# Ten of 22 pairs of the last product with seven block products, their weight sums made earlier and kept in DRAM

## The chip, the cores and the metric

The kernel runs on one core of one Trainium2 chip. The metric is the device time of one execution in microseconds (us). Several runs were timed; their median counts. One more execution was recorded by the hardware profiler, and all views below come from it.

## The reference, cut to what matters

One decoder block on 256 tokens of width 2048, in float32: a norm, two token mixers side by side, an output projection with a residual, then a SwiGLU feed-forward and a final norm. The change concerns the feed-forward alone:

```
h2 = rms_norm(x, norm2_w)                                   # 256 x 2048
x  = x + (silu(h2 @ w_gate) * (h2 @ w_up)) @ w_down         # 5632 wide inside
return rms_norm(x, norm_f_w)
```

`w_gate` and `w_up` are 2048 x 5632, `w_down` is 5632 x 2048. The last product, with `w_down`, is the one that is changed.

## The kernel before, in words

**Three matmuls for one.** Each float32 operand is held as a sum of two parts that TensorE multiplies at its full rate: `hi`, a rounded copy, and `lo`, the rest. A product is hi*hi + hi*lo + lo*hi, so three matmuls stand for each block product. Weights come raw from DRAM and are split in place of use: ScalarE writes `hi` (L161, and L1356 in the last product), VectorE then `lo` = raw - hi (L162, L1357). The tiles `hi` and `lo` are rings of `NH` = 3 buffers of 1024 columns each; a buffer is written again when TensorE has gone through the matmuls that read it. The raw weights lie in a ring of 3 buffers of 2048 columns (1 MB), which SP loads.

**Who sets the order.** The program emits instructions in the order of the code, and a planner then orders each engine's queue by priority and by when it expects the operands. Splits carry a raised priority (`high_priority`), so they run ahead of other work; `pin` keeps an instruction at its place in program order. Side work is written as generators: `add` puts one in a lane, and `pump`, called after each half chunk of weights, advances it by one `yield`.

**Gate/up stage** (L1253 on). For each of 22 groups `g` of 256 inner features, `group_t` computes the gate and the up product, transposed: 256 features by 256 tokens. Four half chunks for each of the two, 24 matmuls of 256 columns per half chunk (L238). The result goes to VectorE (`sgt`), then to one of two places: for a *plain* group, to a hi/lo pair of tiles in `fa`; for a group in `SEVEN` (six of the 22, g = 12 to 17), as float32 into a tile `pairs`.

**Last product** (L1360 on). Two passes p, one for each half of 1024 output columns; a pass runs over the 22 groups ("pairs" of two 128-row blocks of `w_down`).

- A plain pair: four output blocks (two token halves, two column halves c of 512) and two k blocks, three matmuls each, 24 matmuls of 512 columns. They come as two plain halves of 12 (`plain_half`), each with one split of 1024 columns.
- A pair in `SEVEN`: the 2x2 block product by the scheme of Strassen and Winograd, with seven block products instead of eight, 21 matmuls. It needs sums of the left blocks (`sums4`, `sums`, collected by `lefts` into the tiles `left[i]`) and of the weight blocks. `seven_of` makes the weight sums there and then: `d13` on VectorE (L1450), `d24` in two steps on GpSimd (L1451, L1452). It goes in four pieces of 6, 3, 6 and 6 matmuls, and `units` puts a plain half behind each, so that one seven pair is spread over two plain pairs. The products p1, p5, p6, p7 have PSUM banks of their own, which add up over all pairs of a pass.
- The bank set of the products of pass 0 serves pass 1 as accumulators, so `early` empties it at the end of pass 0 into `x1`. `weighted` (L1509) runs in pass 1 on the columns finished in pass 0.
- At the end of pass 1 the splits of the last two plain pairs are made first (`tail`), then their matmuls run sorted by token half, so that the final norm of the first half can start (`add`, `square`, `factor`, `scaled`, L1555 on). One of these splits has a buffer of its own instead of a place in the ring.

Of the kernel before, what the change touches and what calls it, by code (L numbers as in the profile page):

```python
# [7 lines left out]
F32 = mybir.dt.float32  # L8
# [6 lines left out]
P = 128  # L15
# [6 lines left out]
SEVEN = (12, 13, 14, 15, 16, 17)  # L22
# [75 lines left out]
class Kern:  # L98
# [26 lines left out]

    def load(self, src, w, nk=4, parts=None):
        nc = self.nc
        raw = self.wp.tile([P, 2048], F32, tag="raw", bufs=3, name=self.nm("raw"))
        rv = raw[:, :nk * w].rearrange("p (k n) -> p k n", n=w)
        if parts:  # L130

            for i, (k0, k1) in enumerate(parts):
                self.on_load(k0, k1)
                (nc.scalar if i < 2 else nc.sync).dma_start(rv[:, k0:k1, :], src[:, k0:k1, :])
        else:
            nc.sync.dma_start(rv, src)
        return rv

    def split_one(self, rv, w, h, ahead):
# [6 lines left out]
        with self.tc.high_priority(offset=self.HP):  # L146
            for k in range(2):
                self.pin(nc.scalar.activation(hv[:, k, :], rv[:, 2 * h + k, :], AF.Copy))  # L148
                ahead(2 * h + k)
                self.pin(nc.vector.tensor_tensor(lv[:, k, :], rv[:, 2 * h + k, :], hv[:, k, :].bitcast(F32), op=OP.subtract))  # L150
        return hv, lv

    def split(self, rv, w, h, o=0):
        nc = self.nc
        m = rv.shape[1] // 2
# [4 lines left out]
        with self.tc.high_priority(offset=self.HP):  # L160
            nc.scalar.activation(hv, rv[:, m * h:m * h + m, :], AF.Copy)  # L161
            nc.vector.tensor_tensor(lv, rv[:, m * h:m * h + m, :], hv.bitcast(F32), op=OP.subtract)  # L162
        return hv, lv

    def group(self, srcs, acts, w=512, t_outer=False):
# [10 lines left out]
        for c, src in enumerate(srcs):  # L176
            rv = self.load(src, w)
            for h in range(2):
                hv, lv = self.split(rv, w, h)
# [16 lines left out]
    def pair(self, srcs, acts, ws, first):  # L196
# [4 lines left out]
        for c in range(n):  # L201
            for g in range(2):
# [4 lines left out]
                for h in range(2):  # L207
                    if lead:
                        hv, lv = self.split_one(rv, w, h, first.prep0)
                    else:  # L210
                        if g == 0:
                            first.prep(c, h)
                        hv, lv = self.split(rv, w, h)
# [7 lines left out]
    def group_t(self, srcs, acts, out=None):  # L221
# [6 lines left out]
        for c, src in enumerate(srcs):  # L228
            rv = self.load(src, 256, nk=8)
            for h in range(2):  # L230

                hv, lv = self.split(rv, 256, h, 16 * self.nudge)
# [503 lines left out]
    def nsa_kv(self):  # L736
# [36 lines left out]
        for kind in range(2):  # L773
            bank = self.paux.tile([P, 512], F32, tag="acc", bufs=1, name=self.nm("hid"))
            for u in range(2):
                rv = self.load(self.t["w1"][kind * 2 + u], 512)
                for h in range(2):
                    hv, lv = self.split(rv, 512, h)
# [195 lines left out]
    def build(self):  # L974
# [264 lines left out]

        def sums4():  # L1240

            for _ in range(2):
                yield
# [8 lines left out]
        zt = None  # L1252
        for g in range(2 * NFG):  # L1253
            if g == 2 * NFG - 3:
# [7 lines left out]
            if g in SEVEN:  # L1262
                if zt is None:
                    zt = self.xy.tile([P, ZW], F32, tag="z", name="pairs")
                    fp = [zt[:, 512 * o:512 * o + 512] for o in range(6)]
                    z4 = zt[:, 0:2048].rearrange("p (q k t n) -> p q k t n", q=4, k=2, t=2)
                    s4 = [v7(x[:, k]) for x in (pb.tile([P, 2, 512], F32, name=n, tag=n, bufs=1) for n in ("d13", "d24")) for k in range(2)]
                V.tensor_tensor(fp[SEVEN.index(g)].rearrange("p (k n) -> p k n", k=2), e, sgt[:], op=OP.mult)
# [3 lines left out]
            if q % 2 == 0:  # L1272
# [4 lines left out]
                else:  # L1277
                    j = i // 2 - 2
                    if i % 2 == 0:
# [404 lines left out]
```

## Time and profile before

| | |
|---|---|
| median of 3 runs | 1452.66 us (1452.3 to 1454.12) |
| the profiled execution's own time | 1453.31 us |
| its span, first to last instruction | 1451.5 us |
| mean granted TensorE clock | 0.998 |
| gate/up stage | from about 743.5 us to 1211 us of the span |
| last product, pass 0 and pass 1 | from 1211 us; last matmul about 1443 us |

How to read it: PE is TensorE's matmul queue, PEld its weight loads, DVE VectorE, ACT ScalarE, POOL GpSimd, SP the engine that issues most DMAs. A row of instructions gives line, engine, operation and tiles (out<-in), count, then busy time and mean length. A row of waits says which instruction stood idle and which one released it. A row of windows gives the busy time of each engine in a stretch of the span, the granted clock, the busy share of the 16 DMA engines and what they moved. Matmuls overlap in the pipeline, so the length of one (0.39 us for 512 columns) is longer than the distance from one to the next.

### The profile page before, as it was taken

The page shows a single profiled execution, that of the slowest core. Times are in us where ns is not written, and L with a number is a line of the kernel's source. Part 1 is how long each engine was busy: PE and PEld are TensorE (multiplying, and loading weights), DVE is VectorE, ACT ScalarE, POOL GpSimd, SP SyncE. Part 2 cuts the span into 40 slices and gives each one's busy share as a digit, 9 for nine tenths or more (in the row PEclk, how much of TensorE's full clock was granted, in tenths as well). Part 3 has the DMA queues.
Part 4 walks back from the last instruction along what each step waited for, and adds up shares of the span by engine and source line. Part 5 has one row for each costly group of instructions (what it writes and reads, how often), then busy time and mean ns, then how long its engine had stood idle before and what let it go on. Part 6 is the DMA issues. An engine that isn't in the chain of part 4 may idle for free.

```text
span 1451.5 us, 26237 instructions
## 1 busy us (share of the span) xinstructions
PE 1440.7 (99%) x10991; PEld 1377.7 (95%) x10991; DVE 979.7 (67%) x1430; ACT 713.9 (49%) x887; POOL 114.9 (8%) x86
## 2 busy tenths in 40 slices
PE   9999999999999999999999999999999999999997
PEld 9999999999999999998899999999999998888886
DVE  7678997767687755566565555555554558777877
ACT  6655444355455546444454444444444446555555
POOL 1000101000000000120000000000000002221120
PEclk9999999999999999999999999999999999999999
DMA  8665546345554455555555555555555554656653
GB/s 285 231 214 174 177 163 224 121 146 204 203 194 155 146 204 175 183 198 200 175 193 188 200 195 186 200 195 187 200 196 186 200 201 165 216 198 213 209 193 145
DMA packets 48024, 277.12 MB, mean 191 GB/s; under 512 B 5777, under 2 KB 6305, under 8 KB 22049
## 3 DMA queue, kind: packets, MB, share of 16 engines
q1 hardware_dynamic: 45792, 269.56, 53.4%
q10 hardware_dynamic: 1008, 3.25, 0.6%
q0 software_dynamic: 1104, 2.64, 0.6%
q8 instruction: 86, 1.41, 0.4%
q14 instruction: 34, 0.27, 0.1%
HBM read 272.52 MB, written 2.89 MB: 190 GB/s over the span
## 4 chain that ended last, share of the span: by engine, by line
PE 84%; DVE 3%; DMA 0%; issue 0%; ACT 0%; DVEq 0%; ACTq 0%
PE mm L238 56%; PE mm L1369 5%; PE mm L1370 5%; PE mm L1368 5%; PE mm L266 3%; PE mm L265 3%; PE mm L264 3%; DVE lo L162 1%; PE oacc L931 1%; PE U L601 1%; PE mmx L1369 1%; PE mmx L1370 1%; PE mmx L1368 1%; DVE main L403 0%; DVE xs L497 0%; PE pt L917 0%
## 5 line engine op out<-in xcount | busy, mean ns | idle before, releaser
L162 DVE TENSOR_TENSOR lo<-raw,hi 128x1024 fp32r<-128x1024 f32 (+2 forms) x422 | 508.4, 1206 | 297.6 <-ACT hi L161 296.6
L161 ACT ACTIVATE hi<-raw 128x1024 fp32r<-128x1024 f32 (+2 forms) x422 | 440.3, 1046 | 501.6 <-PE mm L238 386.2
L238 PE MATMUL mm<-h,hi 128*128 128x256 f32 x2816 | 348.5, 276 | 0.0
L238 PEld LDWEIGHTS mm<-h,hi 128*128 128x128 f32 x2816 | 332.6, 188 | 0.1
L238 PE MATMUL mm<-hh,hi 128*128 128x256 f32 x2304 | 291.0, 279 | 0.0
L238 PEld LDWEIGHTS mm<-hh,hi 128*128 128x128 f32 x2304 | 275.2, 188 | 0.6 <-ACT hi L161 0.4
L238 PE MATMUL mm<-h,lo 128*128 128x256 f32 x1408 | 188.3, 276 | 0.0
L238 PEld LDWEIGHTS mm<-h,lo 128*128 128x128 f32 x1408 | 172.7, 188 | 0.0
L238 PE MATMUL mm<-hh,lo 128*128 128x256 f32 x1152 | 155.6, 277 | 0.0
L238 PEld LDWEIGHTS mm<-hh,lo 128*128 128x128 f32 x1152 | 142.5, 188 | 0.0
L1357 DVE TENSOR_TENSOR lo<-raw,hi 128x1024 fp32r<-128x1024 f32 (+1 forms) x87 | 115.5, 1339 | 23.5 <-ACT hi L1356 22.7
L1356 ACT ACTIVATE hi<-raw 128x1024 fp32r<-128x1024 f32 (+1 forms) x87 | 87.0, 999 | 66.8 <-PE mm L1370 42.3
L1260 POOL TENSOR_TENSOR sgt<-sgt,R 128x512 f32<-128x512 f32 x22 | 33.3, 1512 | 530.1 <-ACT sgt L1259 530.1
L265 PE MATMUL mm<-lo,xa 128*128 128x512 f32 x128 | 50.1, 391 | 0.0
L266 PE MATMUL mm<-hi,xa 128*128 128x512 f32 x128 | 50.1, 391 | 0.0
L264 PE MATMUL mm<-hi,xa 128*128 128x512 f32 x128 | 49.8, 389 | 0.0
L1181 POOL TENSOR_TENSOR main<-main 128x512 f32<-128x512 f32 x7 | 15.1, 2163 | 379.1 <-DVE main L1180 379.1
L264 PE MATMUL mm<-hi,hh 128*128 128x354 f32 (+2 forms) x128 | 44.0, 351 | 0.8 <-ACT hi L148 0.8
L265 PE MATMUL mm<-lo,hh 128*128 128x354 f32 (+2 forms) x128 | 44.3, 346 | 0.1
L266 PE MATMUL mm<-hi,hh 128*128 128x354 f32 (+2 forms) x128 | 43.8, 343 | 0.0
L1369 PE MATMUL mm<-lo,fa 128*128 128x512 f32 x112 | 43.7, 390 | 0.0
L1368 PE MATMUL mm<-hi,fa 128*128 128x512 f32 x112 | 43.6, 389 | 0.0
(430 smaller groups left out, 1748.2 us busy)
## 6 DMA issues: line engine op xcount, KB each, us to landing
raw<-in_wfg SPq DMA_DIRECT2D x88, 1024.0 KB, 4.8
raw<-in_wd SPq DMA_DIRECT2D x88, 512.0 KB, 4.3
raw<-in_wmg SPq DMA_DIRECT2D x32, 1024.0 KB, 4.8
raw<-in_wdn SPq DMA_DIRECT2D x24, 1024.0 KB, 4.8
raw<-in_nsa SPq DMA_DIRECT2D x16, 1024.0 KB, 4.8
raw<-in_wo SPq DMA_DIRECT2D x16, 1024.0 KB, 4.8
raw<-in_wud SPq DMA_DIRECT2D x8, 1024.0 KB, 4.8
raw<-in_wun SPq DMA_DIRECT2D x8, 1024.0 KB, 4.8
```

What stands on the lines that cost most here:

```text
L161: nc.scalar.activation(hv, rv[:, m * h:m * h + m, :], AF.Copy)
L162: nc.vector.tensor_tensor(lv, rv[:, m * h:m * h + m, :], hv.bitcast(F32), op=OP.subtract)
L238: nc.tensor.matmul(ps[:, f], (hv, hv, lv)[p][:, k, f * P:f * P + P], a[:, p % 2, :], start=c + h + p + k == 0, stop=c == n - 1 and h + p + ...
L264: nc.tensor.matmul(o, a[:, 0, sl], hv[:, k, :], start=begin, stop=False)
L265: nc.tensor.matmul(o, a[:, 0, sl], lv[:, k, :], start=False, stop=False)
L266: nc.tensor.matmul(o, a[:, 1, sl], hv[:, k, :], start=False, stop=last)
L1260: nc.gpsimd.tensor_tensor(sgt[:], sgt[:], self.R2b, op=OP.mult)
L1356: nc.scalar.activation(hv, v, AF.Copy)
L1357: V.tensor_tensor(lv, v, hv.bitcast(F32), op=OP.subtract)
L1368: nc.tensor.matmul(bank, ahi, hv[:, k, :], start=begin, stop=False)
L1369: nc.tensor.matmul(bank, ahi, lv[:, k, :], start=False, stop=False)
L1370: nc.tensor.matmul(bank, alo, hv[:, k, :], start=False, stop=last)
```

## The change

- `SEVEN` has ten groups, in this order: 18, 19, 10, 11, ..., 17. Twelve pairs remain plain. Each pass runs through a written order, `ORDER`: two plain pairs, then eight times a seven pair and a plain pair, two seven pairs, two plain pairs.
- A seven pair now runs in one go, as four pieces of 6, 6, 6 and 3 matmuls with splits of 1024, 1024, 1024 and 512 columns.
- Its weight sums are no longer made there. A generator `staged` in the gate/up stage takes each of the 20 units (10 groups, 2 passes): loads its four blocks on ScalarE's DMA queue (two loads of 512 KB into one of two halves of a tile), four VectorE subtractions of 128x512, and a store of 1 MB to a DRAM tile `scrD`. The last product loads the sums from there: seven blocks per seven pair in five DMAs, where four blocks in two came before.
- The raw ring has 6 buffers of 1024 columns instead of 3 of 2048; every load of weights in the kernel is issued as two DMAs.
- The left operands of groups 18 and 19 are made in the gate/up stage (`one_left`), those of the other eight in pass 0; places of the tiles change with them.

The core of the diff:

```diff
-SEVEN = (12, 13, 14, 15, 16, 17)
+SEVEN = (18, 19, 10, 11, 12, 13, 14, 15, 16, 17)
+ORDER = "PP" + "SP" * 8 + "SSPP"
...
+    def raw(self):
+
+        return self.wp.tile([P, 1024], F32, tag="raw", bufs=6, name=self.nm("raw"))
...
     def load(self, src, w, nk=4, parts=None):
         nc = self.nc
-        raw = self.wp.tile([P, 2048], F32, tag="raw", bufs=3, name=self.nm("raw"))
-        rv = raw[:, :nk * w].rearrange("p (k n) -> p k n", n=w)
+        m = nk // 2
+        rv = [self.raw()[:, :m * w].rearrange("p (k n) -> p k n", n=w) for _ in range(2)]
...
         else:
-            nc.sync.dma_start(rv, src)
+            for h in range(2):
+                nc.sync.dma_start(rv[h], src[:, m * h:m * h + m, :])
...
+        def wd(p, g, c):
+            return t["wd"][(2 * p + c) * NFG + g // 2][:, g % 2 * 2:g % 2 * 2 + 2]
+
+        scrD = self.dram.tile([2, len(SEVEN), P, 4, 512], F32, name="scrD")
+        units = [(p, i) for p in range(2) for i in range(len(SEVEN))]
+
+        def staged():
+
+            yt = self.xy.tile([P, XW[1]], F32, tag="y", name="stage")
+            bufs = [yt[:, 2048 * j:2048 * j + 2048].rearrange("p (k n) -> p k n", n=512) for j in range(2)]
+
+            def into(u):
+                p, i = units[u]
+                for c in range(2):
+                    self.pin(nc.scalar.dma_start(bufs[u % 2][:, 2 * c:2 * c + 2], wd(p, SEVEN[i], c)))
+
+            into(0)
+            for u, (p, i) in enumerate(units):
+                b = bufs[u % 2]
+                for _ in range(3):
+                    yield
+                V.tensor_tensor(b[:, 0], b[:, 2], b[:, 0], op=OP.subtract)
+                V.tensor_tensor(b[:, 2], b[:, 3], b[:, 2], op=OP.subtract)
+                yield
+                V.tensor_tensor(b[:, 3], b[:, 3], b[:, 0], op=OP.subtract)
+                V.tensor_tensor(b[:, 1], b[:, 1], b[:, 3], op=OP.subtract)
+                if u + 1 < len(units):
+                    into(u + 1)
+                yield
+                yield
+                self.pin(nc.scalar.dma_start(scrD[p, i], b))
...
+        def one_left(i, v, cuts):
+
+            z1 = v.rearrange("p (k t n) -> p k t n", k=2, t=2)
+            s = v7(temp("s"))
+            sums((z1[:, 0, 0], z1[:, 0, 1], z1[:, 1, 0], z1[:, 1, 1]), [s[:, m] for m in range(4)])
+            yield
+            (hi, lo), put = cuts
+            put(hi, lo, 0, 2, z1[:, :, 0])
+            put(hi, lo, 2, 3, z1[:, 1, 1].unsqueeze(1))
+            yield
+            put(hi, lo, 3, 7, s)
+            yield
...
+        zt = yl = None
+        self.add(staged())
         for g in range(2 * NFG):
-            if g == 2 * NFG - 3:
+            if g == 18:
...
             if g in SEVEN:
+                i = SEVEN.index(g)
+                if i < 2:
+                    if yl is None:
+                        yl = self.xy.tile([P, XW[1]], F32R, tag="y", name="leftsy")
+                    V.tensor_tensor(sgt[:], e, sgt[:], op=OP.mult)
+                    o = 1792 * i
+                    hl = v7(yl[:, o:o + 896]), v7(yl[:, o + 896:o + 1792])
+                    left[i] = blocks(*hl)
+                    for _ in one_left(i, sgt[:].rearrange("p a b -> p (a b)"), (hl, put)):
+                        pass
...
-            own = [temp("own") for _ in range(2)]
+            yield
+            d2 = pb.tile([P, 2048], F32R, name="dd2", tag="dd", bufs=1)
+            hl = v7(d2[:, 0:896]), v7(d2[:, 896:1792])
+            left[6] = blocks(*hl)
+            yield from one_left(6, fp[4], (hl, put))
+            own = [temp("own") for _ in range(3)]
+            for q in range(3):
+                nc.scalar.activation(own[q], fp[5 + q], AF.Copy)
+            yield
+            z2 = self.xy.tile([P, ZW], F32R, tag="z", name="comb2")
...
             for q in range(2):
-                nc.scalar.activation(own[q], fp[4 + q], AF.Copy)
...
+                o = 1792 * q
+                hl = v7(z2[:, o:o + 896]), v7(z2[:, o + 896:o + 1792])
+                left[7 + q] = blocks(*hl)
+                yield from one_left(7 + q, own[q], (hl, put))
...
-                hi, lo = (pb.tile([P, 1024], F32R, name=self.nm(n), tag=n, bufs=1) for n in ("d13", "d24"))
+                both = pb.tile([P, 2048], F32R, name="dd3", tag="dd", bufs=1)
+                hi, lo = both[:, 0:1024], both[:, 1024:2048]
...
-            def weights(g):
-                raw = self.wp.tile([P, 2048], F32, tag="raw", name=self.nm("raw"))
-                rv = raw[:].rearrange("p (k n) -> p k n", n=512)
-                for c in range(2):
-                    nc.sync.dma_start(rv[:, 2 * c:2 * c + 2, :], t["wd"][(2 * p + c) * NFG + g // 2][:, g % 2 * 2:g % 2 * 2 + 2, :])
-                return rv
+            def chunk(*srcs):
+                rv = self.raw()[:].rearrange("p (k n) -> p k n", n=512)
+                k = 0
+                for src in srcs:
+                    m = src.shape[1]
+                    nc.sync.dma_start(rv[:, k:k + m], src)
+                    k += m
+                return rv[:, 0:k]
...
+            NP = len(plain)
+
+            def plain_unit(q):
+                for c in range(2):
+                    w = halved(chunk(wd(p, plain[q], c)), p == 1 and q == NP - 2 and c == 0)
+                    if p == 1 and q >= NP - 2:
+                        tail[q, c] = w
+                    else:
+                        four_of(q, c, w, last=q == NP - 1)
+                    if q or c:
+                        self.pump()
...
+            def seven_unit(i):
+
+                g, scr = SEVEN[i], scrD[p, i]
+                end = i == len(SEVEN) - 1
+                p1, p5, p6, p7 = prod
                 hi, lo = left[i]
-                L = lambda bank, m, w, k, last=False: mm3(bank, hi[:, m, :], lo[:, m, :], w, k, last)
-                end = i == 5
-                p1, p5, p6, p7 = prod
-                w = halved(sv[:, 0:2, :])
+                L = lambda bank, m, w, k, last=False: mm3(bank, hi[m], lo[m], w, k, last)
+                w = halved(chunk(wd(p, g, 0)))
                 L(p1, 0, w, 0, end)
                 L(acc[0], 1, w, 1)
-                yield
-                w = halved(sv[:, 3:4, :])
+                self.pump()
+                w = halved(chunk(wd(p, g, 1)[:, 1:2], scr[:, 1:2]))
                 L(acc[1], 6, w, 0)
-                d13 = pb.tile([P, 2, 512], F32, name="d13", tag="d13", bufs=1)
-                d24 = pb.tile([P, 2, 512], F32, name="d24", tag="d24", bufs=1)
-                with tc.high_priority(offset=self.HP):
-                    V.tensor_tensor(d13[:], sv[:, 2:4, :], sv[:, 0:4:2, :], op=OP.subtract)
-                self.pin(nc.gpsimd.tensor_tensor(d24[:, 0, :], sv[:, 3, :], d13[:, 0, :], op=OP.subtract))
-                self.pin(nc.gpsimd.tensor_tensor(d24[:, 1, :], sv[:, 1, :], d24[:, 0, :], op=OP.subtract))
-                yield
-                w = halved(d13)
+                L(acc[2], 2, w, 1)
+                self.pump()
+                w = halved(chunk(scr[:, 0:4:2]))
                 L(p5, 3, w, 0, end)
                 L(p7, 5, w, 1, end)
-                yield
-                w = halved(d24)
+                self.pump()
+                w = halved(chunk(scr[:, 3:4]))
                 L(p6, 4, w, 0, end)
-                L(acc[2], 2, w, 1)
                 if end and p == 0:
                     self.add(early())
...
+            def run(order, q, i):
+                for what in order:
+                    if what == "P":
+                        plain_unit(q)
+                        q += 1
+                    else:
+                        seven_unit(i)
+                        i += 1
...
-                units(range(16))
+                run(ORDER, 0, 0)
...
-            units(range(14))
+            run(ORDER[:-2], 0, 0)
...
-            units((14, 15))
+            run(ORDER[-2:], NP - 2, len(SEVEN))
```

More of the change, by code (lines that the diff above doesn't have):

```diff
@@ L133, in load @@
                 self.on_load(k0, k1)
[L134 to L136 removed]
+                h = k0 // m
+                (nc.scalar if i < 2 else nc.sync).dma_start(rv[h][:, k0 - m * h:k1 - m * h, :], src[:, k0:k1, :])
+        else:
+            for h in range(2):
+                nc.sync.dma_start(rv[h], src[:, m * h:m * h + m, :])
         return rv
@@ L1238, in sums, with parts, blocks, put @@
             V.tensor_tensor(s[3], a12, s[1], op=OP.subtract)
+        def wd(p, g, c):
[24 more added lines that the diff above has]
+                self.pin(nc.scalar.dma_start(scrD[p, i], b))
+        def parts(hi, lo, v):
+            nc.scalar.activation(hi, v, AF.Copy)
+            V.tensor_tensor(lo, v, hi.bitcast(F32), op=OP.subtract)
+        left = {}
+        def blocks(hi, lo):
+            return [hi[:, m] for m in range(7)], [lo[:, m] for m in range(7)]
+        def one_left(i, v, cuts):
[9 more added lines that the diff above has]
+            yield
+        def put(hi, lo, m0, m1, v):
+            parts(hi[:, m0:m1], lo[:, m0:m1], v)
         def sums4():
-            for _ in range(2):
-                yield
             a, b = z4[:, :, 0], z4[:, :, 1]
@@ L1287, in build @@
         ct_ = pb.tile([P, 8240], F32R, tag="h2", name="comb")
-        left = [(v7(ct_[:, 1792 * q:1792 * q + 896]), v7(ct_[:, 1792 * q + 896:1792 * q + 1792])) for q in range(4)]
+        for q in range(4):
+            left[2 + q] = blocks(v7(ct_[:, 1792 * q:1792 * q + 896]), v7(ct_[:, 1792 * q + 896:1792 * q + 1792]))
         c4 = ct_[:, 0:7168].rearrange("p (q l m n) -> p q l m n", q=4, l=2, m=7)
-        def parts(hi, lo, v):
-            nc.scalar.activation(hi, v, AF.Copy)
-            V.tensor_tensor(lo, v, hi.bitcast(F32), op=OP.subtract)
         def lefts():
@@ L1461, in seven_of @@
                 if end and p == 0:
                     self.add(early())
-                yield
-            def units(qs):
-                s7 = None
-                for q in qs:
-                    i, second = (q - begin7) // 2, (q - begin7) % 2 == 1
-                    pair = 0 <= i < 6
-                    if pair and not second:
-                        s7 = seven_of(i)
-                        next(s7)
-                    rv = weights(plain[q])
-                    for c in range(2):
-                        if pair:
-                            next(s7)
-                        plain_half(rv, q, c)
+            def run(order, q, i):
[6 more added lines that the diff above has]
+                        i += 1
```

72 lines of the change are left out of this document (27 added, 45 removed).

## The prediction

> **What bounds the kernel now.** I read the page's busy times first, then who waited on TensorE, then the last product by stretches, then single instructions there.
>
> ```profile
> span 1451.5 us, 26237 instructions
> PE 1440.7 (99%) x10991; PEld 1377.7 (95%) x10991; DVE 979.7 (67%) x1430; ACT 713.9 (49%) x887; POOL 114.9 (8%) x86
> ...
> raw<-in_wd SPq DMA_DIRECT2D x88, 512.0 KB, 4.3
> ```
> ```profile
> PE idle L1003 <- POOL ones L996: 0.9, 1, 0.9
> PE mm L264 <- ACT hi L148: 0.8, 1, 0.8
> PE qtr L544 <- ACT main L407: 0.6, 1, 0.6
> ```
> ```profile
> core 0: us, PE busy (x) PEld busy (x) DVE busy (x) ACT busy (x) POOL busy (x), PEclk, DMA share, GB/s
> 743.50:1070.00 326.50, 326.50 (x2882) 326.50 (x2881) 172.76 (x163) 145.55 (x148) 22.91 (x15) 1.00 0.56 194
> 1211.30:1322.00 110.70, 110.70 (x490) 91.46 (x490) 87.87 (x81) 59.93 (x69) 26.08 (x12) 1.00 0.59 200
> 1322.00:1432.00 110.00, 110.00 (x487) 91.10 (x486) 88.41 (x81) 59.24 (x66) 21.24 (x12) 1.00 0.59 199
> ```
> TensorE is busy 99% of the span, and its three waits on other engines lie in the first 220 us. The last three rows are the gate/up stage and the two passes (p = 0, 1) of the last product: TensorE runs through at full granted clock (1.00), VectorE at 53% and then 80%, DMA at 0.56 and 0.59. So matmuls taken out shorten the span one for one, as long as nothing else makes TensorE wait; nearly nothing does today. How close it comes is seen at one spot (the timeline's columns are start, length, instruction):
>
> ```profile
> 1240.54 4.95 DVE L1357 TENSOR_TENSOR lo<-raw,hi 128x1024 fp32r<-128x1024 f32 x3 [0.17 <-ACT hi L1356]
> ...
> 1243.32 0.39 PE L1368 MATMUL mm<-hi,comb 128*128 128x512 f32 x1
> ...
> 1243.52 0.63 ACT L1356 ACTIVATE hi<-raw 128x512 fp32r<-128x512 f32 x1 [1.66 <-PE mm L1370]
> ...
> 1244.68 0.39 PE L1368 MATMUL mm<-hi,fa 128*128 128x512 f32 x1
> ...
> 1244.93 0.19 PEld L1369 LDWEIGHTS mm<-lo,fa 128*128 128x128 f32 x1 [0.29 <-DVE lo L1357]
> ...
> 1245.27 0.39 PE L1370 MATMUL mm<-hi,fa 128*128 128x512 f32 x1
> ```
> Three things are read here. The six matmuls (L1368, L1369, L1370, twice) of a piece on `comb` take 1243.32 to 1244.68: 0.2267 us each. A conversion by ScalarE starts 0.20 us after the piece that held its buffer has given way to the next (1243.52 against 1243.32), because hi and lo are rings of three (NH = 3). And a lo half that ends late holds the weight load of L1369: it started at 1244.93 where the matmul before it had started at 1244.68, and L1370 came at 1245.27, 0.34 later, where 1244.68 + 0.45 = 1245.13 was due. From the load to its matmul are thus 0.34 - 0.23 = 0.11 us, and TensorE lost 0.14.
>
> **The change, part by part.**
>
> *Matmuls.* Before: 2 passes x (16 plain pairs x 24 + 6 pairs x 21) = 1020; after: 2 x (12 x 24 + 10 x 21) = 996. 24 x 0.2267 = **5.44 us less**, all on the path.
>
> *The order in the last product.* Before, a pair of seven products was cut in four pieces (6, 3, 6, 6 matmuls), and a plain half (12) stood behind each. Now a pair runs in one go, A, B, C of 6 and D of 3 matmuls (1.36, 1.36, 1.36, 0.68 us), then the two plain halves. Durations of what must keep up:
>
> ```profile
> L1356 ACT ACTIVATE hi<-raw x87: 632/1061/1067, 1205.2 to 1432.0; 128x1024 fp32r<-128x1024 f32 x75, 128x512 fp32r<-128x512 f32 x12
> L1357 DVE TENSOR_TENSOR lo<-raw,hi x87: 679/1219/2385, 1206.3 to 1433.4; 128x1024 fp32r<-128x1024 f32 x75, 128x512 fp32r<-128x512 f32 x12
> ```
> With three buffers the plain half behind D takes the buffer of B. Counted from B's end: hi starts at 0.22, ends at 1.28, lo ends at about 2.53; 0.05 to the load and 0.11 to the matmul give 2.70. Without a wait, D ends at 1.36 + 0.68 = 2.04, and the half's second matmul, the first to read lo, is due at 2.27. It is **0.43 us late, at every pair**. Before, two pieces in a row last 3.4 us at least (3 + 12 matmuls), so the same sum had 0.9 us to spare. If the order written for TensorE puts the other bank's hi matmul (L1368) first, as it may, 0.2267 of that is filled and 0.21 stays. The same holds for C (2.72 + 0.23 against 2.70): just in time. So: 10 pairs in pass 0, 9 in pass 1 (its last is followed by a half with its own buffer): 19 x 0.21 = **4.1 us** or 19 x 0.43 = **8.2 us**. I take 4.1; before's order never had such a case, so both ends stay.
>
> *POOL's two subtractions and L1450 leave the last product.*
>
> ```profile
> L1450 DVE TENSOR_TENSOR d<-raw 128x1024 f32<-128x1024 f32 x12 | 14.7, 1222 | 3.5 <-DMA raw<-in_wd 3.4
> ```
> VectorE loses 14.7 us and the slow lo halves (2385 ns, beside POOL's), but only the 0.14 us above was on the path: **-0.14**. Per pair and plain unit VectorE then has 5 x 1.22 + 0.69 = 6.8 us of splits in the 10.2 us of TensorE (45 matmuls): the rate suffices, only the moment is late.
>
> *Left operands.* Four pairs, not two, get theirs in pass 0; each adds on VectorE four sums of 128x128 (0.29, as the parts of that size) and lo parts of 0.42, 0.29 and 0.69 us, 2.6 us.
>
> ```profile
> L1293 DVE TENSOR_TENSOR comb<-own,comb x4: 287/356/424, 1222.7 to 1226.1; 128x256 fp32r<-128x256 f32 x2, 128x128 fp32r<-128x128 f32 x2
> ...
> L1293 DVE TENSOR_TENSOR comb<-s,comb x2: 686/1238/1789, 1223.2 to 1228.5; 128x512 fp32r<-128x512 f32 x2
> ```
> The first pair starts after 10.9 us, not 16.3, so these ops fall between splits that now have no slack. A 0.69 us op ahead of a late lo costs up to that; at one or two of the first five pairs, **+0.6** (0 to 2). The same for the four weightings in pass 1 (L1509, 1237 ns, held in program order) and the sums between the passes: **+0.7** (0 to 3).
>
> ```profile
> L1509 DVE TENSOR_TENSOR x1t<-x1t,wf 128x512 f32<-128x512 f32 x4 | 4.9, 1237 | 0.0
> ```
> *The end.* Today a plain half (2.72 us) stands between the last product and the closing halves; VectorE uses it:
>
> ```profile
> 1428.57 0.68 DVE L1521 TENSOR_TENSOR x1t<-mm,x1t 128x512 f32<-128x512 f32 x1
> ...
> 1436.43 0.69 DVE L1563 TENSOR_TENSOR x1t<-v,x1t 128x512 f32<-128x512 f32 x1
> 1437.54 1.29 DVE L1534 TENSOR_TENSOR x1t<-mm,x1t 128x512 f32<-128x512 f32 x2 [0.43 <-PE mm L1370]
> ...
> 1440.11 0.21 DVE L1543 TENSOR_SCALAR sstf<-ssf,sstf 128x1 f32<-128x1 f32 x1 [0.87 <-ACT root L1548]
> ```
> Afterwards the two pairs come right before the closing halves, so two lo halves (2.4 us) move into the time before the first L1534; it slips by about 2 us, of which the idle time there and behind it (0.43 and 0.87) takes 1.3, and the closing halves may wait another 0.6 for lo. **+1.3** (0 to 3).
>
> *Weight sums in gate/up.* 20 units of a 1 MB load, four VectorE subtractions of 128x512 (half of L1450's 1222 ns, so some 0.69 each) and a 1 MB store, one per 6 pumps of 2.72 us. VectorE: 80 x 0.69 = 55 us in 326, from 53% to 70%. ScalarE: 60 issues, about SP's 0.33 each, so 20 us more on 45% busy. A unit's load has 5 pumps, 13.6 us, to land; its buffer's store 4 pumps. L1450 above stood 3.4 us in all for its DMA; if VectorE or ScalarE so wait for a staged transfer, the splits queued behind wait too:
>
> ```profile
> 1001.20 1.06 ACT L161 ACTIVATE hi<-raw 128x1024 fp32r<-128x1024 f32 x1 [1.61 <-PE mm L238]
> 1002.29 1.22 DVE L162 TENSOR_TENSOR lo<-raw,hi 128x1024 fp32r<-128x1024 f32 x1 [1.45 <-ACT hi L161]
> ```
> hi starts when half n's 16 hi matmuls are through, lo ends 2.3 us later, and is read first after 16 matmuls of half n+2, some 4.7 us after that. That slack covers them: **0**; uncovered, 0.5 us x 20 = 10.
>
> *Half-size buffers and DMA.* Raw loads become two of 512 KB; SP issues twice per 5.44 us in gate/up, and in the last product 5 loads per pair and 2 per plain unit, 7 x 0.38 = 2.7 us of 10.2 (0.33 to 0.38 by the row). The last product now needs 2.75 MB per 10.2 us = 283 GB/s, not 200, in gate/up 194 + 2.1 MB/16.3 us = 322.
>
> ```profile
> L1388 SPq DMA_DIRECT2D raw<-in_wd x88: 327/375/1161, 1194.0 to 1420.5; - x88
> ```
> ```profile
> 0.00:20.00 20.00, 18.21 (x95) 16.70 (x96) 13.96 (x29) 13.32 (x23) 3.80 (x7) 1.00 0.90 324
> 1383.50:1393.50 10.00, 10.00 (x45) 8.29 (x45) 6.81 (x7) 4.55 (x5) 0.00 (x0) 1.00 0.80 289
> ```
> Both rates have been reached: 324 at share 0.90, 289 at 0.80 with 512 KB pieces. Six buffers give a raw load some 7.5 us in the last product and 13 in gate/up, against 4.3 to land: **0** (-0.5 at the start of the kernel by earlier releases, to +11, below).
>
> The Trainium skill (DMA: Bandwidth & Descriptors, Measured) says to batch to 1 MiB or more for 75% of peak, and its fit of 2.0 us plus bytes at 436 GB/s puts a lone 512 KB load at an estimated 164 GB/s, under what either stage needs. By it alone both stages would starve; 289 GB/s with such pieces shows that overlapping loads escape it.
>
> *Sum*: -5.44 - 0.14 + 4.1 + 0.6 + 0.7 + 1.3 = **+1.1 us**. The profiled execution took 1453.31 (span 1451.5 and 1.8 around it), 0.65 above the median 1452.66: 1454.4 against it, **1453.8** against the median.
>
> **Rivals.** A difference under 0.2% (2.9 us) can't be told from none.
> - *Slower: the lo wait isn't filled.* If TensorE's order stays hi, lo, hi per bank (as in all of before's last product), each pair costs 0.43: +1.1 + 4.1 = +5.2, **1457.9**; with the upper ends of the smaller terms 1462. It decides from 0.31 us per pair on (19 x 0.31 = 5.9, with the other terms +2.9). For: the arithmetic leaves no slack. Against: a planner that sees lo late can reorder. 0.30.
> - *Faster: no such wait.* If conversions come earlier than I count, say because a single-block piece frees its buffer sooner, -5.44 plus about 0.6 of small terms: **1447.8**. For: no such wait exists before. Against: the 1.66 us for which ScalarE waited for TensorE ahead of its hi above; it starts when it may. 0.20.
> - *DMA binds in gate/up.* 322 GB/s is 0.93 of the engines' share at 194 GB/s per 0.56. If only 312 are to be had, 3% of 326 us is lost: +10, **1464**. For: 0.90 at 324 is the most seen. Against: 13 us of slack per load. 0.08. The skill's page (the Trainium skill, same page, Where 436 GB/s comes from) puts a core's HBM share at about 358 GB/s; no run so far shows that limit.
>
> **How the numbers follow.** Forecast, gain eaten by the lo waits, 1450 to 1455.5: 0.42. Slower: 0.30 + 0.08 = 0.38. Faster: 0.20. The range for 8 in 10 goes from within the faster case, 1448, to the upper end of the unfilled wait, 1462; each side leaves about 0.1.
>
> **What would show it.** 24 fewer matmuls of 512 columns; in the last product, TensorE weight loads of the lo matmul waiting for lo some 0.2 to 0.4 us about 19 times, at the first plain half behind each pair; no POOL there; lo means back at 1.22; gate/up still 326.5/2882 = 113 ns per matmul at DMA share 0.9. The forecast is wrong if those waits are missing (then near 1448), or if the gate/up matmuls stretch.

## The result, and the profile after

The changed kernel takes 1466.78 us (median of 5 runs, 1462.32 to 1471.36), the kernel before 1452.66 (5 runs, 1452.18 to 1454.12): a ratio of 1.0098, 95% interval 1.0072 to 1.0125. The forecast was 1453.8, in a range of 1448 to 1462: the time came out above it. The profiled execution took 1466.78, its span is 1465.0. From its page:

```profile
span 1465.0 us, 27053 instructions
...
PE 1448.7 (99%) x10967; PEld 1379.0 (94%) x10967; DVE 1015.0 (69%) x1539; ACT 725.7 (50%) x913; POOL 67.6 (5%) x62
```
TensorE has its 24 matmuls less, is still busy 99%, and is busy 8 us longer. So look where it stalls and how fast it steps. By first and last matmul of the stages in the two traces (gate/up counted from its first matmul, 12.5 us ahead of the 743.5 us given with the profile before), the 13.5 us of span come from:

| | before | after | difference |
|---|---|---|---|
| gate/up begins | 730.95 | 728.45 | -2.5 |
| gate/up stage | 480.40 | 493.29 | +12.9 |
| last product, first to last matmul | 231.46 | 231.07 | -0.4 |
| last matmul to the end | 8.74 | 12.20 | +3.5 |

The waits of the last product in the changed kernel (what waited on whom: us in total, times, longest):

```profile
PEld mm L1448 <- DVE lo L1436: 6.7, 19, 0.6
```
The count is the forecast's, and so are all but one of the places: 18 of these waits lie at the first half or piece behind a pair of seven. At the 19th such place (1248.8 us) TensorE waited for hi instead, and the list's 19th lo wait is in the closing halves. By the step from matmul to matmul these waits cost 4.2 us over the pace, 0.19 us at most of the places. The waits of gate/up:

```profile
DVE stage L1268 <- DMA stage<-in_wd: 46.3, 11, 6.8
...
PEld mm L245 <- DVE lo L169: 3.8, 6, 1.0
...
PE mm L245 <- DVE lo L169: 2.4, 5, 0.8
```
VectorE stands 46.3 us for staged loads, and TensorE, which had no such wait before, waits for lo. One of these places, on VectorE and on TensorE's weight load (start, length, instruction, idle time before it):

```profile
978.53 1.22 DVE L169 TENSOR_TENSOR lo<-raw,hi 128x1024 fp32r<-128x1024 f32 x1 [1.49 <-ACT hi L168]
985.67 0.69 DVE L1268 TENSOR_TENSOR stage<-stage 128x512 f32<-128x512 f32 x1 [5.92 <-DMA stage<-in_wd]
986.28 1.22 DVE L169 TENSOR_TENSOR lo<-raw,hi 128x1024 fp32r<-128x1024 f32 x1
987.42 0.69 DVE L1269 TENSOR_TENSOR stage<-stage 128x512 f32<-128x512 f32 x1
988.14 0.69 DVE L1271 TENSOR_TENSOR stage<-stage 128x512 f32<-128x512 f32 x1
988.86 0.69 DVE L1272 TENSOR_TENSOR stage<-stage 128x512 f32<-128x512 f32 x1
989.47 0.68 DVE L1321 TENSOR_TENSOR sgt<-mm,R 128x512 f32<-128x512 f32 x1
990.07 1.22 DVE L169 TENSOR_TENSOR lo<-raw,hi 128x1024 fp32r<-128x1024 f32 x1
```
```profile
991.34 1.00 PEld L245 LDWEIGHTS mm<-h,lo 128*128 128x128 f32 x8 [0.54 <-DVE lo L169]
```
The load was issued at 974.72. VectorE waits 5.92 us for it with two lo halves behind it, then makes the sums and a product as well, and the second lo half ends about 991.3, half a microsecond too late. What follows is the larger loss. By stretches (length, busy time and count of TensorE, its weight loads, VectorE, ScalarE, GpSimd; granted clock, DMA share, GB/s), first the changed kernel, then the kernel before:

```profile
800.00:850.00 50.00, 50.00 (x444) 50.00 (x443) 32.25 (x36) 21.33 (x22) 3.09 (x2) 1.00 0.91 317
...
992.00:1022.00 30.00, 30.00 (x257) 30.00 (x256) 18.00 (x19) 12.91 (x13) 1.98 (x2) 1.00 0.93 330
...
1100.00:1150.00 50.00, 50.00 (x427) 50.00 (x426) 24.45 (x22) 19.84 (x20) 3.49 (x3) 1.00 0.57 190
```
```profile
1100.00:1150.00 50.00, 50.00 (x443) 50.00 (x443) 26.42 (x25) 21.21 (x22) 2.96 (x2) 1.00 0.55 193
```
427 matmuls in 50 us in place of 443, with no wait, at full granted clock, and also when the staging is over (its last store was issued at 1065.6 us) and DMA is back at 0.57. From start to start the step is 113.3 ns up to the stall at 990.7 us and 117.8 ns for some 1950 matmuls from there to the last product: 8.7 us. At 800 us the step was right, at DMA share 0.91. With the stalls (at six places, 0.4 to 1.1 us each, 4.2 us more than before) that is gate/up's 12.9. Not every stall has this effect: behind the four earlier ones (791.7, 855.2, 858.4 and 924.7 us), three of them longer than this one, the step was 113.3 ns again.

The end of the chain that ended last:

```profile
1437.08 1.24 DVE lo L1436
1438.33 5.96 DMA raw<-in_wd
1444.39 1.07 ACT hi L1435
1445.49 1.23 DVE lo L1436
1446.71 0.61 DVE u L1590
1447.35 0.69 DVE w L1591
...
1451.16 0.61 DVE x1t L1602
```
The last raw half could be loaded only when a lo half had freed its buffer at 1438.3, 14.5 us ahead of the last matmul. It landed 8.5 us ahead of it, and VectorE's sums for the output queue up behind it; before, the last loads were issued at 1420, 22 us ahead of the last matmul.

### The profile page after: what moved, and what is told of

The parts are those of the page before. It is cut to its first block, busy times and chain, and to the rows that moved or that the text cites. A ratio compares the mean times of both kernels' runs of the same rounds, so it can differ in the third digit from the quotient of the medians.

```text
span 1465.0 us, 27053 instructions
## 1 busy us (share of the span) xinstructions
PE 1448.7 (99%) x10967; PEld 1379.0 (94%) x10967; DVE 1015.0 (69%) x1539; ACT 725.7 (50%) x913; POOL 67.6 (5%) x62
## 5 line engine op out<-in xcount | busy, mean ns | idle before, releaser
L245 PE MATMUL mm<-h,hi 128*128 128x256 f32 x2816 | 354.3, 278 | 0.0
L245 PEld LDWEIGHTS mm<-h,hi 128*128 128x128 f32 x2816 | 338.0, 188 | 0.1
L245 PE MATMUL mm<-h,lo 128*128 128x256 f32 x1408 | 191.9, 279 | 2.6 <-DVE lo L169 2.4
L1436 DVE TENSOR_TENSOR lo<-raw,hi 128x1024 fp32r<-128x1024 f32 x127 | 141.3, 1139 | 64.8 <-ACT hi L1435 62.5
L1435 ACT ACTIVATE hi<-raw 128x1024 fp32r<-128x1024 f32 x127 | 123.9, 990 | 90.7 <-PE mm L1449 66.2
L1268 DVE TENSOR_TENSOR stage<-stage 128x512 f32<-128x512 f32 x20 | 13.8, 692 | 70.3 <-DMA stage<-in_wd 46.3
```

Of the source, the lines that this page charges most:

```text
L245: nc.tensor.matmul(ps[:, f], (hv, hv, lv)[p][:, k, f * P:f * P + P], a[:, p % 2, :], start=c + h + p + k == 0, stop=c == n - 1 and h + p + ...
L1435: nc.scalar.activation(hv, v, AF.Copy)
L1436: V.tensor_tensor(lv, v, hv.bitcast(F32), op=OP.subtract)
```

## The experiments

Times are medians, and each ratio is to runs of before that were made beside it; the other columns are of each kernel's profiled execution. "Slow" counts gate/up matmuls (of 4224) that start 116 to 125 ns after the one before; some 35 are normal.

| kernel | time | ratio to before (95%) | gate/up | slow | last product | end |
|---|---|---|---|---|---|---|
| before | 1452.66 | | 480.40 | 34 | 231.46 | 8.7 |
| changed | 1466.78 | 1.0098 (1.0072 to 1.0125) | 493.29 | 1991 | 231.07 | 12.2 |
| e1_half_buffers | 1452.95 | 0.9998 (0.9988 to 1.0007) | 480.40 | 36 | 233.70 | 8.5 |
| e2_nudge | 1464.69 | 1.0079 (1.0064 to 1.0094) | 488.72 | 955 | 231.20 | 11.8 |
| e3_no_sums | 1454.38 | 1.0009 (0.9999 to 1.0018) | 480.40 | 36 | 230.67 | 12.1 |
| e4_no_staging | 1454.68 | 1.0010 (1.0000 to 1.0019) | 480.40 | 34 | 230.61 | 12.3 |
| f1_sums_on_gpsimd | 1460.36 | 1.0059 (1.0036 to 1.0082) | 485.37 | 634 | 230.62 | 11.5 |
| f2_sums_later | 1466.99 | 1.0090 (1.0055 to 1.0125) | 496.14 | 3143 | 230.59 | 11.7 |
| f3_hi_first | 1461.21 | 1.0048 (1.0031 to 1.0066) | 492.10 | 2147 | 226.47 | 12.0 |
| g1_sums_later_pinned | 1454.67 | 1.0011 (1.0001 to 1.0021) | 480.40 | 34 | 230.82 | 12.2 |
| g2_pool_queue_hi_first | 1450.78 | 0.9983 (0.9974 to 0.9992) | 480.40 | 35 | 226.46 | 11.7 |
| g3_pool_queue_hi_first_order | 1449.19 | 0.9974 (0.9965 to 0.9984) | 480.40 | 34 | 228.55 | 8.8 |
| h2_order_P_SP10_P | 1448.51 | 0.9970 (0.9959 to 0.9980) | 480.40 | 34 | 226.21 | 10.7 |
| h3_order_SSPSPP | 1449.61 | 0.9976 (0.9966 to 0.9986) | 480.40 | 36 | 226.98 | 10.9 |
| i1_long_delays_same_layout | 1467.78 (one run) | | 494.96 | 627 | 231.29 | 8.8 |
| i2_small_tiles_only | 1496.56 (one run) | | 502.72 | 3381 | 234.66 | 8.8 |

**Parts of the change alone.** e1 is the kernel before with `raw` in six halves:

```
-        raw = self.wp.tile([P, 2048], F32, tag="raw", bufs=3, ...)
+        return self.wp.tile([P, 1024], F32, tag="raw", bufs=6, ...)
```


> The kernel before with one part of the change: raw weights in six buffers of 1024 columns in place of three of 2048, each half loaded by a DMA of its own. (The one subtraction that spans both halves of a pair becomes two of 512 columns each.) Between the two traces gate/up began 2.5 us earlier after the change (728.45 against 730.95 us). Theory: that gain is the half-size buffers', because a buffer comes free after one half, and they cost nothing later: 1452.7 - 2.5 = 1450.2 us. Rival: the 2.5 us belong to something else and twice as many DMAs cost as much as they bring: 1452.7 us. Rival 2: the half-size buffers themselves make the gate/up stage longer (12.9 us longer after the change): 1463 us.

The rival's 1452.7 us came, the theory's 1450.2 did not: gate/up began at 729.95, 1.0 us earlier, and the last product was 2.2 us longer (mostly two lo waits, 0.7 and 1.2 us). Over the kernels here with half-size buffers gate/up began anywhere from 728.5 to 731.4, so the 2.5 us between the first two traces are mostly scatter. The buffers are worth nothing either way.

e3 leaves the sums out, e4 the staging:

```
 e3  -                V.tensor_tensor(b[:, 0], b[:, 2], b[:, 0], op=OP.subtract)   # and the other three
 e4  -        self.add(staged())
     -                w = halved(chunk(scr[:, 0:4:2]))
     +                w = halved(chunk(wd(p, g, 1)))                               # and the other two
```


> The changed kernel with the staging's loads and stores, but without its 80 VectorE subtractions: the scratch in DRAM then holds the raw weights (so the weight sums of the last product are left out), the DMA traffic is the same in every stage. Theory: VectorE, which stands at a subtraction until the staged load lands (46.3 us of waits in 11 rows), delays the lo halves, and the stalls and the slow step follow from that: gate/up back to about 480.5 us with 113.3 ns throughout, time about 1454 us. Rival: the extra DMA traffic (share 0.90 in gate/up) delays the weights or slows TensorE by itself: gate/up near 493 us, time near 1466.8 us.

> The changed kernel without any staging in gate/up; the last product reads raw blocks of the same size from the weights in place of the stored sums (so the sums are left out). All theories that put the loss in gate/up on the staging expect gate/up at 480.4 us as before, the last product at 231 us, the end 3.5 us late as in the changed kernel: 1452.7 - 2.5 - 0.4 + 3.5 = 1453.3 us. What lies between this kernel and the one with the loads and stores alone is the price of the DMA traffic: 0 to 1 us by the first theory, up to 13 us by the rival. If gate/up is long here too, the half-size buffers are to blame: 1466 us.

The theory held. e3, in the same stretch of gate/up:

```profile
1000.00:1050.00 50.00, 50.00 (x444) 50.00 (x443) 28.03 (x28) 21.40 (x22) 4.57 (x3) 1.00 0.89 316
```
All the staged traffic runs, 316 GB/s, and TensorE steps at 113 ns without a stall. DMA costs nothing here; the subtractions on VectorE, with the waits that they bring, cost it all.

**The slow step.** e2 makes the kernel's own shift of a lo tile once per group:

```
         for g in range(2 * NFG):
+            self.nudge = True
             e = self.group_t([t["wfg"][g * 4 + c] for c in range(2)], h2)
```


> The changed kernel, but at the start of each of the 22 gate/up groups one lo tile is shifted by 16 elements (the kernel's own nudge, which it otherwise makes after transposes). In the trace of the changed kernel the gate/up matmul's step goes from 113.3 to 117.7 ns at one stall (990.7 us, 0.5 us long) and stays there for 230 us, 1957 matmuls: 8.5 us. Theory: the slow step is a state of TensorE's that a stall can start and a shifted operand ends; then it lasts at most one group (about 22 us, 0.8 us), gate/up falls from 493.3 to about 485.5 us and the time from 1466.8 to about 1459 us, with less spread between runs. Rival: the slow step is made by the staged DMA traffic or by VectorE's load on the SBUF; then the shift changes nothing: 1466.8 us.

Right in kind, too high in size, and by time alone it can't be told from the changed kernel (1463.16 to 1465.92 us against 1462.32 to 1471.36). Four of its six stalls, 0.4 to 1.0 us each, were followed by the slow step. Three of these spells ended at a shift and one at the next stall, but two shifts in the middle of a spell did nothing. One spell and a stretch between two:

```profile
863.00:890.00 27.00, 27.00 (x232) 27.00 (x231) 17.78 (x19) 11.99 (x13) 1.54 (x1) 1.00 0.97 351
900.00:925.00 25.00, 25.00 (x222) 25.00 (x221) 13.98 (x17) 9.66 (x10) 1.54 (x1) 1.00 0.92 314
```
From start to start the step is 117.8 against 113.6 ns, at 351 and 314 GB/s. Gate/up came down to 488.7, not 485.5: 3.9 us of stalls more than before stayed, and some 760 slow matmuls in spells.

To see whether a stall alone does it, f4 and g4 put 18 and 24 short subtractions ahead of six lo halves of the kernel before; the build spread them over gaps, TensorE never stalled (1452.87 and 1453.24 us), and they said nothing on the step.

> The kernel before with six delays in gate/up and no staging: ahead of one lo half in groups 2, 5, 8, 11, 14 and 17 VectorE makes 18 idle subtractions of 256 columns, 0.35 us each, 6.3 us against the 4.7 us by which lo is early. If a stall of TensorE alone starts the slow step (117.7 ns in place of 113.3), some of these six stalls are followed by it until another stall ends it: between 0 and 16 us besides 6 x 1.6 us. If the slow step needs the staged DMA traffic, all matmuls outside the stalls stay at 113.3 ns and gate/up grows by about 10 us at most.

> The kernel before with the six delays lengthened from 18 to 24 subtractions of 256 columns (0.35 us each, 8.4 us); 18 of them made no stall, so lo is more than 6.3 us early. If a stall of TensorE alone starts the slow step, some of the six stalls (about 1 us each) are followed by matmuls at 117.7 ns until a later stall ends it: gate/up 5 to 20 us longer. If it needs the staged DMA traffic or the sums, 113.3 ns everywhere outside the stalls: gate/up at most 8 us longer, all of it in the stalls.

h1 used one long instruction each, but took 1521.32 us: all was slow from the start, and the suspicion fell on its small result tiles, which move the tiles behind them. So i1 repeats it with the result elsewhere, and i2 has the tiles alone (the lines are shortened, with names put in):

```
 h1  +   V.tensor_reduce(self.small([5]), x1t[:, 0:1, :].to_broadcast([P, 5, 2048]), ...)
 i1  +   V.tensor_reduce(pb_tile[:, 0:17], x1t[:, 0:1, 0:512].to_broadcast([P, 17, 512]), ...)
 i2  +   V.memset(self.small([5], self.nm("jam"))[:], 0.0)
```


> The kernel before, no staging, with one long VectorE instruction ahead of a lo half in groups 2, 5, 8, 11, 14 and 17: a sum over 5 x 2048 elements, about 10.7 us by the 1.22 us that 1024 elements take, which cannot be spread over several gaps as the short ones were. The lo halves ran up to 7 us early, so TensorE should stall 1 to 4 us, six times. Theory: a stall of TensorE alone can start the slow step, so behind some of the six the matmuls go on at 117.7 ns until a later stall, or the last product, ends it: 3 to 20 us more than the stalls. Rival (the slow step needs the staged DMA traffic or the sums): 113.3 ns outside the stalls.

> The kernel before with the six long VectorE instructions, now a sum over 17 x 512 elements (about 9.2 us by the 10.81 us that 10240 took), and its result in the last pool, so that no other tile moves in SBUF. In the run before this one six small result tiles had moved the tiles behind them, and all matmuls from the start ran slow (119 to 120 ns in gate/up ahead of the first delay). Theory: gate/up starts at 113.3 ns; six stalls of 0.6 to 1.8 us; behind some of them 117.7 ns until a later stall ends it, 3 to 15 us more. Rival (only the staging's traffic or sums starts the slow step): 113.3 ns outside the stalls and the 3 us behind each, in which the step was 213 ns; gate/up at most 15 us longer, all of it there.

> The kernel before with only the six small tiles (5 numbers each, written once) and no delay. Theory: the matmul's step depends on where the operands lie in SBUF, and the six tiles move every tile of the pools behind them; then the whole kernel runs at the slow step as in the run with six long delays: gate/up begins near 749 us (18 us late) and steps 119 to 120 ns, about 506 us long; time 1453 + 18 + 26 + 2 = about 1499 us. Rival (the slowness there came from the program, not from the tiles' places): 1453 us.

i1 stalled at 787.8, 854.6, 921.5, 990.9, 1054.5 and 1123.7 us, 0.8 to 2.2 us each. Behind the third the step was 117.8 ns, and the fourth ended that:

```profile
925.00:990.00 65.00, 65.00 (x554) 65.00 (x553) 39.58 (x32) 27.07 (x29) 4.89 (x3) 1.00 0.54 191
995.00:1050.00 55.00, 55.00 (x487) 55.00 (x487) 31.06 (x28) 23.67 (x24) 4.91 (x3) 1.00 0.60 216
```
From start to start 117.8 and 113.3 ns, without any staging, in this one execution. So a stall alone can start the slow step, though five of the six didn't, and another can end it. i2:

```profile
850.00:900.00 50.00, 50.00 (x424) 50.00 (x423) 26.03 (x25) 21.30 (x23) 3.23 (x3) 1.00 0.53 182
```
Six tiles of five numbers, written once in the first microsecond and read by nothing, cost 44 us: the step is 118.7 ns for 256 columns all through gate/up (not the 119 to 120 of the expectation). That leaves the places of the operands, which the tiles shift; no view shows the places themselves. Why a place or a stall sets the step was not found out.

**Where the sums are made.** All three change `staged` alone: f1 moves the subtractions to GpSimd and holds them in place there, f2 adds a step, and g1 is f2 with the subtractions held in place (of four lines, the first is shown):

```
 f1  -                V.tensor_tensor(b[:, 0], b[:, 2], b[:, 0], op=OP.subtract)
     +                self.pin(nc.gpsimd.tensor_tensor(b[:, 0], b[:, 2], b[:, 0], op=OP.subtract))
 f2  -                for _ in range(3):
     +                for _ in range(4):
 g1  +                for _ in range(4):
     +                self.pin(V.tensor_tensor(b[:, 0], b[:, 2], b[:, 0], op=OP.subtract))
```


> The changed kernel with the 80 staged subtractions on GpSimd in place of VectorE, in the same places of the program. Theory: what costs in gate/up is that VectorE stands at a subtraction until its load lands while a lo half waits behind it; GpSimd has one product of 1.51 us per group there and can wait, so gate/up falls from 493.3 to about 480.5 us and the time to that of the kernel without subtractions, 1454.4 us. Rival: the subtractions cost by their work on the SBUF, whoever makes them (GpSimd slows VectorE's lo and ScalarE's hi): gate/up stays above 485 us, time above 1459 us.

> The changed kernel with one step more (2.7 us) between the issue of a staged load and the first VectorE subtraction on it; the staging then ends at about 1120 us instead of 1066. Waits for staged loads were 46.3 us in 11 rows, 4.2 us each, the longest 6.8 us. Theory (VectorE stands at the subtraction until the load lands, TensorE stalls only where that is over the 4.7 us by which the lo half is early): 2.7 us less wait in each leaves the longest at 4.1 us, few or no stalls in gate/up, no slow step, time 1454 to 1458 us. Rival (it is VectorE's extra work of 4 x 0.69 us in a row that delays a lo half, not the wait): the same stalls, 1463 to 1470 us.

> The kernel with one step more before the staged subtractions, and the 80 subtractions now held on VectorE at their place in the program; without that, the build had put the first one 9 to 11 us behind the issue of its load whatever the program said, and it waited for the load all 20 times (71.9 us). Held, it comes two or three lo halves later, some 5 to 8 us. Theory (the wait for the load is the cause): no waits of VectorE for staged loads, no stall in gate/up, 113.3 ns throughout: gate/up about 480.5 us, time about 1454.5 us, as without subtractions. Rival (four subtractions, 2.76 us, ahead of a lo half are too much): stalls and the slow step as before, 1460 to 1471 us.

f1 came out at its rival's figures, but mainly by another wait: ScalarE, which issues the stores, now stood ahead of a hi half until GpSimd was done. The rival has a share that was not separated: VectorE's lo took 1426 ns on average in gate/up, against 1237 in the changed kernel. f1's waits, then f2's:

```profile
ACT hi L168 <- POOL stage L1272: 39.8, 7, 6.7
```
```profile
DVE stage L1268 <- DMA stage<-in_wd: 71.9, 20, 6.4
```
f2 looked like the rival's win and was not: the step in the program did not move the instruction. The subtraction is not pinned in `staged`, and VectorE still came to it 4.6 to 7.6 us behind the issue of its load (3.8 to 7.7 in the changed kernel). The data was there only 5.5 to 11.1 us behind the issue, so it waited all 20 times. The issue of one unit's two loads and its first subtraction, in f2 and in g1:

```profile
805.93 0.82 ACTq L1261 DMA_DIRECT2D stage<-in_wd  x2
...
816.95 0.69 DVE L1268 TENSOR_TENSOR stage<-stage 128x512 f32<-128x512 f32 x1 [5.63 <-DMA stage<-in_wd]
```
```profile
804.75 0.82 ACTq L1261 DMA_DIRECT2D stage<-in_wd  x2
...
823.29 0.68 DVE L1268 TENSOR_TENSOR stage<-stage 128x512 f32<-128x512 f32 x1
```
Pinned (g1), VectorE comes to it 16 to 19 us behind the issue (10.8 the first time), not the 5 to 8 that were expected. The wait is gone from the list, and gate/up takes 480.40 us, to the hundredth that of before, with all 80 subtractions on VectorE:

```profile
1000.00:1050.00 50.00, 50.00 (x444) 50.00 (x443) 32.75 (x36) 21.50 (x22) 3.92 (x3) 1.00 0.87 314
```
So the wait was the cause, not the work (VectorE 66% busy here, 56% in e3). The pins also held the step that f2 had added; whether they would do without it was not run. f1 and f3 have the same gate/up program and the same 2.3 us of stalls more than before, with 634 and 2147 slow matmuls: that is probably also why the changed kernel's runs lie 9 us apart.

**The last product.** f3 puts f1's matmuls in the order that reads hi first; g2 adds that order to g1 and issues the staged DMAs from GpSimd:

```
-                nc.tensor.matmul(bank, ahi, lv[:, k, :], start=False, stop=False)
-                nc.tensor.matmul(bank, alo, hv[:, k, :], start=False, stop=last)
+                nc.tensor.matmul(bank, alo, hv[:, k, :], start=False, stop=False)
+            for bank, ahi, alo, k, last in todo:
+                nc.tensor.matmul(bank, ahi, lv[:, k, :], start=False, stop=last)
```


> The kernel with the sums on GpSimd, and in the last product the matmuls of a half in another order: first all that read hi, then those that read lo (gate/up has that order already). In the trace of the changed kernel the matmul that reads lo waits at the first plain half behind each pair of seven, 19 times, 0.21 us each, 4.2 us over the pace. Theory: with 8 instead of 1 or 2 matmuls ahead of the first lo these waits are covered: last product 231.1 - 4 = 227 us, time 4 us below the kernel with the sums on GpSimd. Rival: the waits only move to the hi of the next half, because the ring of three hi and lo tiles is the limit: 231 us.

> The same as the pinned kernel, with the staged loads and stores issued by GpSimd's queue in place of ScalarE's, and the last product's matmuls in the order that reads hi first. With the subtractions on GpSimd, ScalarE stood 39.8 us (7 times, up to 6.7 us) before a hi half, at a store that waited for the sums; GpSimd has only its product per group to delay. Theory: gate/up 480.4 us, last product 226.5 us, so 1453.5 less 4.2 = about 1450 us. Rival: GpSimd's product now comes late behind a store or a load, VectorE waits for it with a lo half behind it, and gate/up is 485 us or more: 1455 us or more.

In the last product both came as the theory said: 230.62 to 226.47 us. f3's time did not fall with it (1461.21 against 1460.36), because its gate/up was 6.7 us longer; g2's did. TensorE's only wait for lo left in f3's last product:

```profile
PEld mm L1451 <- DVE lo L1436: 0.4, 1, 0.4
```
The order of the units, on top of g2:

```
-ORDER = "PP" + "SP" * 8 + "SSPP"
+ORDER = "SP" * 9 + "SPPP"              # g3
+ORDER = "P" + "SP" * 10 + "P"          # h2
+ORDER = "PP" + "SP" * 7 + "SSPSPP"     # h3
```


> The same again, with the units of the last product in the order SP x 9, S, PPP (S a pair with seven products, P a plain pair) in place of PP, SP x 8, SSPP: no two S in a row, and a plain pair between the last S and the closing halves. In the changed kernel the last raw half landed at 1444.3 us, 8.5 us before the last matmul, and VectorE worked off its sums behind it: 12.2 us from the last matmul to the end against 8.7 before. Theory: the end is late because the last weights are, and VectorE's queue with them; with this order the end takes 8.7 us again and the time is 3 us below the kernel with the old order. Rival: the left operands of the first S are not ready so early and pass 0 starts with stalls that cost as much: no gain.

> The pinned kernel with GpSimd's queue and hi first, and the last product's units in the order P, SP x 10, P: no two S in a row, closing halves behind the last S. With S-P x 9, S, PPP the end fell from 11.7 to 8.8 us, but TensorE stalled 2.3 us in the last product, 0.36 at the start of pass 1 (S first) and 1.3 us at 1419 us at the last S. Theory: the end is late because two S in a row (3.6 MB in 9.5 us) drain the six raw buffers; without them the last loads come earlier: end 9 to 10 us, last product 226.5 to 227 us, time 1448.5 us. Rival: the end is late because no plain pair stands between the last S and the closing halves: end 11.7 us, time 1450.8 us.

> The same with the order PP, SP x 7, SSP, SPP: two plain pairs first as in the changed kernel, two S in a row one plain pair earlier, a single S before the closing halves. Theory of the drained buffers: the SS still drains them, the plain pair behind it refills only part; end 10 to 11.7 us, last product 226.5 us, 1449 to 1450 us. Rival (no plain pair behind the last S): end 11.7 us, 1450.8 us.

Neither theory of the end was the whole of it. Taking the two S apart (h2) or moving them (h3) brings 11.7 to 10.7 and 10.9; only the plain pair behind the last S as well (g3) brings 8.8, and there TensorE stalled 2.3 us elsewhere. h2 is the fastest kernel here: 0.9970 of before, with an interval of 0.9959 to 0.9980.

## Why the prediction was wrong, by its steps

- *Weight sums in gate/up, "that slack covers them: 0".* This step failed, by 12.9 us. The slack was there: in the trace of before lo ends 4.8 to 6.2 us ahead of the first matmul that reads it. But the step weighed against it the 3.4 us in all for which L1450 had stood. The waits were up to 6.8 us each, and the sums (2.76 us) and a product (0.68) come on top of them on the same queue. The "13.6 us to land" was read from the program's steps, while the build puts an instruction that is not pinned where it likes: at 974.72 the load is issued, at 979.75 VectorE is at the subtraction, at 985.67 it can start. g1, where the steps hold, has the forecast's 0. The forecast had named the sign of this failure itself: gate/up's matmuls stretched.
- *"Uncovered, 0.5 us x 20 = 10".* Near in size by accident: the stalls were 4.2 us, at six places. The other 8.7 are the slow step, which the prediction did not know. It had stood in the trace of before: 24 matmuls of 256 columns stepped at 118 ns behind four short ones (L1067, 743 us), and the 12 of 512 columns that read the tile with a buffer of its own stepped at 233. The kernel even has a shift (`nudge`) that moves a lo tile.
- *DMA binds (1464).* Near the time, wrong in mechanism: e3 has the traffic, 0.89 and 316 GB/s, and loses nothing.
- *Matmuls, -5.44, and the lo wait, +4.1.* Right: 24 fewer, and 4.2 us of waits at the places named, filled by the other bank's matmul and not 8.2. f3, without these waits, is 4.2 us shorter than f1 in the last product.
- *Left operands and weightings, +0.6 and +0.7.* Right in sum by luck: with them the last product was to change by -0.2, and it changed by -0.4. No wait of that kind is in its list; instead 177 of its matmuls step 230 to 240 ns, where 26 did before, and that costs 1.0 us.
- *The end, +1.3.* Mis-sized: +3.5. It counted the two lo halves that move, and took their loads to be on time; the orders above show that the late loads and the missing plain pair share it.
- *Half-size buffers, 0.* Right: e1 0.9998.

With gate/up as forecast, g1 takes 1454.67, 0.9 us over the forecast, of which the end's excess is 2.2.

## What to carry to other kernels

Before an instruction that waits for a DMA is put on an engine with work that others need, look at what stands behind it on that engine, add the instruction's own time to the wait, and hold it at a place where the data has surely landed; giving a later place in the program is not enough if the build may move it. After any stall, compare the step from matmul to matmul before and behind it: half a microsecond was followed by 8.7 us of slower steps, and longer stalls before it by none. Where a product needs a part that is made late, put all matmuls that do not read that part first.

## What was not expected of the hardware

At a granted clock of 1.00, a matmul of 256 columns steps at 113.3 or 117.8 ns (118.7 in i2, with other places of the operands), and can stay so for over 200 us until a stall or a shifted operand changes it. The Trainium skill (TensorE: Matmul & The Clock Gate, Wait — 56ns, not 53.3ns?) gives columns / 2.4 GHz plus a fixed 2.5 ns, an estimated 109.2 ns here; the traces differ, with a second addition that the page does not have. And a stall of 2.2 us at 1054.5 us in i1 was followed by 3.4 us at half clock, an equal one at 1123.7 by none:

```profile
1056.90:1060.30 3.40, 3.40 (x16) 3.40 (x17) 3.38 (x3) 2.12 (x2) 0.00 (x0) 0.51 0.37 92
```
In h1 three of four stalls of 2.3 us were followed by half clock and one was not. Its spells of half clock last 3.41 us (one 6.83) and begin a whole number of 3.413 us apart: 71.68 us twice (21 of them), 139.95 (41) and 75.09 (22). The same page of the Trainium skill (What's actually happening) has half clock follow an idle window of about 3.4 us that runs freely. The lengths and distances agree with that; that a stall of 2.2 us can be enough is what these two runs add, and what decides it stays open.
